# One transformer block on one core: matmul passes that read their 512 weight columns alternately from two halves

## The chip, the core and the metric

The kernel runs on one core of a Trainium2 chip. Each core has a matrix engine (TensorE; PE in the profile, with PEld for its loading of the stationary operand), VectorE (DVE), ScalarE (ACT), GpSimd (POOL) and SyncE (SP), which here only starts transfers. The metric is the device time of one execution in microseconds. Before the change it is 292.63 us, the median of 3 runs (292.62 to 293.44).

## The reference

One block of depth 1 on an input of 256 tokens by 1024 channels, all in 32-bit floats. Cut to what matters:

```python
u = rms_norm(h, mix_norm_g[l])
proj = u @ w_in[l]                                  # 1024 x 2560
q, k, v, glu_a, glu_g = jnp.split(proj, splits, axis=-1)
attn_out = moba_attention(heads(q), heads(k), heads(v), rel_bias)
conv_out = conformer_conv(glu_a, glu_g, conv_w[l], conv_b[l], conv_ln_g[l], conv_ln_b[l])
h = h + jnp.concatenate([attn_out, conv_out], axis=-1) @ w_out[l]
u = rms_norm(h, ffn_norm_g[l])
h = h + (jax.nn.silu(u @ w_gate[l]) * (u @ w_up[l])) @ w_down[l]
return rms_norm(h, final_norm_g)
```

The feed-forward width is 2816, so gate and up are 1024 x 2816 each and down is 2816 x 1024. With 256 tokens the attention has a single block, and is plain causal attention with a position bias, 8 heads of 64.

## The kernel before

**Split weights, three passes.** Each weight arrives as 32-bit floats in a tile `raw` (128 x 1024). `high` (line 138) rounds it on ScalarE to a tile `wh` of the shorter float type fp32r, and `split` (line 158) subtracts on VectorE, leaving the rest in a part `wl` of one long tile, `low`. Activations are split likewise (`uh`, `ul` and `hh`, `hl`, all within the tile `us`; `fh`, `fl` for the feed-forward's products). A product is three passes of TensorE into one accumulator: high by high, high by low, low by high. `cut` (line 165) gives the columns of `wh` and `wl` for a pass.

**Which operand moves.** A pass holds one operand of 128 columns still and streams the other through. For q, k, the convolution's inputs and the output projection the weights are held and 256 columns of activations move. For values (`v_mm`, line 460), gate and up (`up_mm`, line 579) and down (`down`, line 636) the activations are held, 128 tokens at a time, and **512 columns of weights move**; the result has tokens on its partitions. Down has a few passes of 256 columns too, at the very end (accumulator `pe`).

**The columns' layout.** The host function `_layout` (line 794) arranges the weights. For values a row holds 8 stretches of 512 columns, one for each 128 input channels. For gate and up such a stretch is 256 columns of gate followed by 256 of up, for one group of the feed-forward width; for down it is half of a row of 1024. Each pass reads its 512 columns one after another, 4 bytes each.

**Order.** Up to the feed-forward part the order of the work is written out by hand in `PROGRAM` (line 43), a list of steps; each engine runs its steps in that order. The values' steps `v.0` to `v.3` stand among the steps of the softmax and the convolution; each is 12 passes. Then 11 groups follow (line 673): for group g, `swiglu` turns the accumulators `pf` of gate and up into products `ff`; `gate_up` issues the 48 passes of the next group (8 blocks of input channels, 2 blocks of tokens, 3 passes each); the 24 passes of `down` for group g - 1 follow, into the four accumulators `pd`; the splits of the weights for two groups later are queued on ScalarE and VectorE. All passes are recorded at line 74 (transposes at line 77) and all instructions of the other engines at line 85, so that the tiles' names tell them apart. At the end (line 697) the last three down groups are ordered by token half, with the residual sum, the final norm and the output behind each half.

**Transfers.** Weights come in transfers of 512 KB (256 KB for the first ones) on SyncE's queue, into 6 `raw` buffers, two for each weight; `wh` has 9 buffers and `wl` 9 places.

Of the kernel before, what the change touches and what calls it, by code (L numbers as in the profile page):

```python
# [15 lines left out]
P = 128  # L16
S = 256
D = 1024
# [43 lines left out]
def block_kernel(ctx, tc, xT, w_in, w_out, w_gu, w_down, pvec, gfin, relb, hot, out):  # L62
# [10 lines left out]
    def mm(*args, **kw):  # L73
        return tc.keep_in_program_order(nc.tensor.matmul(*args, **kw))  # L74
# [14 lines left out]
    def bank(i, name):  # L89
        return psum.tile([P, 512], F32, tag=f"b{i}", name=name)  # L90
# [15 lines left out]
    raws, parts = {}, {}  # L106
# [58 lines left out]
    def cut(name, c, n):  # L165
        return [w[:, c % HW : c % HW + n] for w in parts[name][c // HW]]


    def mm3(o, name, c, uh, ul, start, stop):
        wh, wl = cut(name, c, P)  # L170
        mm(o, wh, uh, start=start, stop=False, skip_group_check=True)
        mm(o, wh, ul, start=False, stop=False, skip_group_check=True)
        return mm(o, wl, uh, start=False, stop=stop, skip_group_check=True)
# [286 lines left out]
    def v_mm(i):  # L460
        if i == 0:
            pvt.extend(bank(t, f"pv{t}") for t in range(2))
        for k in range(2 * i, 2 * i + 2):
            wh, wl = cut(f"v{k // 4}", (k % 4) * 512, 512)
            for t in range(2):
                tok = slice(t * P, (t + 1) * P)
                mm(pvt[t], uh[:, k, tok], wh, start=k == 0, stop=False)
                mm(pvt[t], uh[:, k, tok], wl, start=False, stop=False)
                mm(pvt[t], ul[:, k, tok], wh, start=False, stop=k == KD - 1)
# [85 lines left out]
    def a0(k):  # L555
# [6 lines left out]
    ops = {"ld": fetch, "zd": bias_out, "bd": bias_in, "ud": stack_out, "us": stack_in, "h": high, "w": split, "rb": row_scale, "hb": bias_parts, "pl": late_columns, "pz": bias_mm, "zs": bias_copy, "vt": v_out, "rs": scale_x, "rd": scale_diagonal, "ca": lambda half: conv_taps(half, 0, 1),  # L562
           "a0": a0, "a1": a1, "glu": glu, "qk": qk_mm, "qo": qk_out, "sc": score, "t": logits, "n": normed, "fl": flip,
           "fo": flip_out, "v": v_mm, "pv": pv_mm, "mo": mix_out, "l": norm, "o": o_mm, "f": finish, "c": conv,
           "co": conv_out, "cw": conv_weights, "ct": conv_taps, "hs": lambda m: sumsq(acch, xs[:, m], m, "h"),
           "sq": lambda k: sumsq(accx, xs[:, k], k, "x"), "g": lambda m: lower_u(m, PV_G2)}
# [10 lines left out]
    pf, ff, acts = {}, {}, {}  # L577

    def up_mm(g, t, k):
        wh, wl = cut("gu"[k // 4] + str(g), k % 4 * 512, 512)  # L580
        tok = slice(t * P, (t + 1) * P)
        mm(pf[g][t], hh[:, k, tok], wh, start=k == 0, stop=False)
        mm(pf[g][t], hh[:, k, tok], wl, start=False, stop=False)
        mm(pf[g][t], hl[:, k, tok], wh, start=False, stop=k == KD - 1)

    def gate_up(g):
        pf[g] = [bank(next(spare), f"pf{g}{t}") for t in range(2)]
        for k in range(KD):
            for t in range(2):
                up_mm(g, t, k)  # L590
# [44 lines left out]

    def down(g, i, t, lo, hi, o=None, start=None, stop=None):
        f = 2 * g + i
        wh, wl = cut(f"d{g}", i * D + lo, hi - lo)
        fh, fl = (a[:, t, i] for a in acts[g])
        if o is None:  # L640
            o = pd[t][lo // 512][:, lo % 512 : lo % 512 + hi - lo]
            start, stop = f == 0, f == (NF - 1 if lo == 0 else NF - 3)
        mm(o, fh, wh, start=start, stop=False, skip_group_check=True)
        mm(o, fh, wl, start=False, stop=False, skip_group_check=True)
        mm(o, fl, wh, start=False, stop=stop, skip_group_check=True)
# [17 lines left out]
    for k in range(KD):  # L663
        for t in range(2):
            up_mm(0, t, k)
        if k == 5:
            rc2 = rstd(acch, D, RMS_EPS, "h", next(spare))
            split("u1")
# [4 lines left out]
    for g in range(FG):  # L673
        swiglu(g)
        if g < FG - 1:
            send(g)
            gate_up(g + 1)
        if g > 0:
            split(f"d{g - 1}")
            land(g - 1)  # L680
        if 0 < g < FG - 2:
            for i in range(2):
                for t in range(2):
                    for n in range(2):
                        down(g - 1, i, t, n * 512, n * 512 + 512)
        if g < FG - 2:
            split(f"g{g + 2}")
            split(f"u{g + 2}")
        if 1 <= g <= 4:
            h_turn(2 * g - 2)  # L690
            h_turn(2 * g - 1)
        if g == 4:
            h_rows()
# [3 lines left out]
    for i in range(2):  # L697
        for t in range(2):
            for n in range(2):
                down(FG - 3, i, t, n * 512, n * 512 + 512)  # L700
        flip_ff(FG - 1, i)

    def last(g, t, lo, hi, *o):
        for i in range(2):
            down(g, i, t, lo, hi, *((o[0], i == 0, i == 1) if o else ()))

    a, b = FG - 2, FG - 1
# [54 lines left out]
def _one_hot():  # L762
    hot = np.zeros((2, NB, S), np.float32)
    hot[:, _buckets(), np.arange(S)] = float(HD) ** 0.5
    return hot.reshape(2 * NB, S)
# [3 lines left out]
def _conv_taps(w):  # L769
    return w[: 4 * Q].reshape(Q, 4, 16, 32).transpose(1, 3, 2, 0).reshape(P, 16 * Q)  # L770


def _pieces(w, fine=0):
    j = [*range(0, fine, HW // 2), *range(fine, w.shape[1] + 1, HW)]
    return np.concatenate([w[:, a:b].ravel() for a, b in zip(j, j[1:])])


def _rows(w):
    k = w.shape[0] // P
    return w.reshape(k, P, w.shape[1]).transpose(1, 0, 2)  # L780
# [3 lines left out]
def _rows_d(w):  # L784
    return w.reshape(4, KD, 32, w.shape[1]).transpose(0, 2, 1, 3).reshape(P, KD, w.shape[1])

def _turned(w):
    g = w[: FF - S].reshape(FG - 1, 4, 2, 32, D).transpose(0, 2, 1, 3, 4).reshape(FF - S, D)  # L790
    return np.concatenate([g, w[FF - S :]], axis=0)


def _layout(x, mix_norm_g, w_in, rel_bias, conv_w, conv_b, conv_ln_g, conv_ln_b, w_out,
            ffn_norm_g, w_gate, w_up, w_down, final_norm_g):
    flat = lambda a: np.ascontiguousarray(a.reshape(P, -1))
    wi = _rows_d(w_in[0])
    q, k, v, a, g = (wi[:, :, i * 512 : (i + 1) * 512] for i in range(5))
    parts = []
    for half in range(2):  # L800
        c = slice(half * S, (half + 1) * S)
        parts.append(np.concatenate([a[:, :, c], g[:, :, c]], axis=2).reshape(P, -1))
    for hp in range(4):
        c = slice(hp * P, (hp + 1) * P)
        parts.append(np.concatenate([q[:, :, c], k[:, :, c]], axis=2).reshape(P, -1))
    parts.append(v.reshape(P, -1))
    pairs = [_rows_d(w[0]).reshape(P, KD, FG, S).transpose(0, 2, 1, 3) for w in (w_gate, w_up)]
    cols = lambda b: b.reshape(-1, P).T
    pvec = np.concatenate(
        [_rows_d(mix_norm_g[0][:, None])[:, :, 0], _rows_d(ffn_norm_g[0][:, None])[:, :, 0], cols(conv_b[0]), cols(conv_ln_g[0]), cols(conv_ln_b[0]),  # L810
         *(cols(w) for w in conv_w[0][4 * Q :]), _conv_taps(conv_w[0]), np.tile(np.eye(32, dtype=np.float32), (4, 1))], axis=1)
    return {
        "xT": np.ascontiguousarray(_rows_d(np.ascontiguousarray(x[0].T)).transpose(1, 0, 2)),
        "w_in": _pieces(np.concatenate(parts, axis=1), 2048 * len(FINE)),
        "w_out": _pieces(flat(_rows(w_out[0].reshape(D, 4, KD, 32).transpose(0, 2, 1, 3).reshape(D, D)))),
        "w_gu": _pieces(flat(np.concatenate(pairs, axis=3))),
        "w_down": _pieces(flat(_rows(_turned(w_down[0])))),
        "pvec": np.ascontiguousarray(pvec),
        "gfin": np.ascontiguousarray(final_norm_g),
        "relb": np.ascontiguousarray(rel_bias),  # L820
        "hot": _one_hot(),
    }
# [17 lines left out]
```

## Time and profile before

| | |
|---|---|
| median of 3 runs | 292.63 us |
| span of the profiled execution | 291.1 us |
| TensorE busy | 283.6 us, 97% of the span |
| VectorE, ScalarE busy | 203.6 us, 156.7 us |
| mean granted clock of TensorE | 0.997 |
| bytes moved by the DMA engines | 63.73 MB, mean 219 GB/s |

The span runs from the first to the last instruction; the profile gives no other time for that execution, and the median of the runs is 1.5 us above the span. "Busy" counts TensorE's passes with a modelled end, and passes overlap, so a busy TensorE need not be at its best pace: the pace is the time from the start of one pass to the start of the next. A group of instructions is listed as line, engine, operation, output<-inputs, shape and count, then busy us, mean ns of one, and idle time before. The granted clock is a share of 2.4 GHz; the other level is 1.2 GHz.

### The profile page before, as it was taken

How to read it: one execution, taken by the hardware profiler on the slowest of the kernel's cores; microseconds unless marked ns; L12 is line 12 of the kernel's file. 1: busy time of each engine (PE TensorE's matmuls, PEld its weight loads, DVE VectorE, ACT ScalarE, POOL GpSimd, SP SyncE). 2: the span in 40 equal slices, each digit the busy share in tenths (PEclk: the TensorE clock that was granted, in tenths of full speed). 3: DMA queues.
4: the chain of work that ended last, by engine and by line, in shares of the span. 5: the costliest groups of instructions: out<-in, count | busy, mean ns of one | idle time of the engine just before them, and what ended most of it. 6: DMA issues, size and time to landing. Idle time of an engine off the chain costs nothing.

```text
span 291.1 us, 4726 instructions
## 1 busy us (share of the span) xinstructions
PE 283.6 (97%) x1717; PEld 243.4 (84%) x1717; DVE 203.6 (70%) x375; ACT 156.7 (54%) x272; POOL 43.6 (15%) x80
## 2 busy tenths in 40 slices
PE   8999999999999999999999999999999999999991
PEld 8999996986799988888888888888888888888881
DVE  3998998999986989859928467381829365411884
ACT  3984668916795577547618173452618172402531
POOL 2000100000000002143211213223221213130000
PEclk9999999999999999999999999999999999999998
DMA  7999799951057447989994949889795949420012
GB/s 221 332 379 335 252 275 252 385 194 55 16 160 260 175 140 205 328 274 303 347 311 148 297 117 321 292 266 356 237 266 172 296 117 325 134 74 0 0 55 89
DMA packets 22089, 63.73 MB, mean 219 GB/s; under 512 B 3178, under 2 KB 5938, under 8 KB 22066
## 3 DMA queue, kind: packets, MB, share of 16 engines
q1 hardware_dynamic: 18754, 54.94, 57.5%
q0 software_dynamic: 2880, 7.95, 9.7%
q10 hardware_dynamic: 432, 0.54, 0.5%
q8 instruction: 13, 0.21, 0.3%
q14 instruction: 10, 0.08, 0.1%
HBM read 58.10 MB, written 5.32 MB: 218 GB/s over the span
## 4 chain that ended last, share of the span: by engine, by line
PE 92%; issue 2%; DVE 2%; DMA 2%; SPq 1%; ACT 1%; POOLq 0%; POOL 0%; DVEq 0%
PE pf L74 41%; PE pd L74 18%; PE py L74 8%; PE pqk L74 8%; PE pv L74 4%; PE pa L74 3%; PE pg L74 3%; PE pc L74 3%; DMA raw_a<-in_w_in 2%; PE pt L77 1%; PE ps L74 1%; PE po L74 1%; DVE ht L85 1%; SPq L85 1%; DVE hg L85 0%
## 5 line engine op out<-in xcount | busy, mean ns | idle before, releaser
L74 PE MATMUL pf<-wl,us 128*128 128x512 f32 x176 | 68.5, 389 | 0.0
L74 PE MATMUL pf<-wh_u,us 128*128 128x512 f32 x176 | 56.2, 390 | 0.0
L74 PE MATMUL pf<-wh_g,us 128*128 128x512 f32 x176 | 56.0, 389 | 0.0
L85 DVE TENSOR_TENSOR ff<-fs,pf 128x256 f32<-128x256 f32 x22 | 9.1, 419 | 55.4 <-ACT fs L85 55.4
L85 ACT ACTIVATE fs<-pf,rc_h 128x256 f32<-128x256 f32 x22 | 10.3, 475 | 67.3 <-PE pf L74 65.8
L74 PEld LDWEIGHTS pf<-wl,us 128*128 128x128 f32 x176 | 33.0, 188 | 6.9
L74 PEld LDWEIGHTS pf<-wh_u,us 128*128 128x128 f32 x176 | 33.0, 188 | 6.8
L74 PEld LDWEIGHTS pf<-wh_g,us 128*128 128x128 f32 x176 | 33.0, 188 | 6.8
L74 PE MATMUL pd<-wh_d,fh 128*128 128x512 f32 x84 | 32.9, 391 | 0.0
L74 PE MATMUL pd<-wh_d,fl 128*128 128x512 f32 x84 | 32.7, 390 | 0.0
L74 PE MATMUL pd<-wl,fh 128*128 128x512 f32 x84 | 32.7, 389 | 0.0
L85 DVE TENSOR_TENSOR wl<-raw_u,wh_u 128x1024 fp32r<-128x1024 f32 x22 | 26.5, 1220 | 8.7 <-ACT wh_u L85 8.7
L85 ACT CAST wh_u<-raw_u 128x1024 fp32r<-128x1024 f32 x22 | 22.8, 1051 | 14.6 <-PE pf L74 10.9
L85 POOL DMA_DIRECT2D fb<-fd x40 | 23.2, 585 | 45.1 <-issue 23.5
L85 DVE TENSOR_TENSOR wl<-raw_g,wh_g 128x1024 fp32r<-128x1024 f32 x22 | 25.9, 1217 | 1.0 <-ACT wh_g L85 1.0
L85 DVE TENSOR_TENSOR wl<-raw_d,wh_d 128x1024 fp32r<-128x1024 f32 x22 | 25.6, 1202 | 0.5 <-ACT wh_d L85 0.5
L74 PE MATMUL pqk<-us,wh_qk 128*128 128x256 f32 x128 | 22.2, 277 | 0.0
L85 ACT CAST wh_g<-raw_g 128x1024 fp32r<-128x1024 f32 x22 | 22.0, 1049 | 0.0
L85 ACT CAST wh_d<-raw_d 128x1024 fp32r<-128x1024 f32 x22 | 21.9, 1047 | 0.0
L74 PEld LDWEIGHTS pqk<-us,wh_qk 128*128 128x128 f32 x128 | 19.4, 188 | 0.5 <-issue 0.4
L74 PEld LDWEIGHTS pd<-wh_d,fl 128*128 128x128 f32 x84 | 15.8, 188 | 3.3
L74 PEld LDWEIGHTS pd<-wl,fh 128*128 128x128 f32 x84 | 15.8, 188 | 3.2
(153 smaller groups left out, 531.9 us busy)
## 6 DMA issues: line engine op xcount, KB each, us to landing
raw_g<-in_w_gu SPq DMA_DIRECT2D x22, 512.0 KB, 5.3
raw_u<-in_w_gu SPq DMA_DIRECT2D x22, 512.0 KB, 6.5
raw_d<-in_w_down SPq DMA_DIRECT2D x22, 512.0 KB, 5.1
raw_qk<-in_w_in SPq DMA_DIRECT2D x8, 512.0 KB, 7.5
raw_o<-in_w_out SPq DMA_DIRECT2D x8, 512.0 KB, 4.2
raw_a<-in_w_in SPq DMA_DIRECT2D x12, 256.0 KB, 4.3
fd<-fv POOLq DMA_DIRECT2D x10, 256.0 KB, 3.9
fb<-fd POOLq DMA_DIRECT2D x40, 64.0 KB, 4.9
```

What stands on the lines that cost most here:

```text
L74: return tc.keep_in_program_order(nc.tensor.matmul(*args, **kw))
L77: return tc.keep_in_program_order(nc.tensor.transpose(o, i, ident))
L85: return lambda *a, **k: tc.keep_in_program_order(f(*a, **k))
```

## The change

In the kernel a view is laid over the 512 columns of a moving weight. `in_turns` takes them as two halves of 256 and walks column 0 of the first half, column 0 of the second, column 1 of the first, column 1 of the second, and so on. On the host `_in_turns` stores the columns of each stretch of 512 so that this walk meets them in their old order: even columns fill the first half and odd ones the second. So the results stand in the same places in the accumulators as before. For down's passes of 256 columns the view is cut to the matching 128 columns of each half.

```diff
+    def in_turns(w):
+        return w.rearrange("p (h a) -> p a h", h=2)
 
@@ v_mm
-            wh, wl = cut(f"v{k // 4}", (k % 4) * 512, 512)
+            wh, wl = map(in_turns, cut(f"v{k // 4}", (k % 4) * 512, 512))
@@ up_mm
-        wh, wl = cut("gu"[k // 4] + str(g), k % 4 * 512, 512)
+        wh, wl = map(in_turns, cut("gu"[k // 4] + str(g), k % 4 * 512, 512))
@@ down
-        wh, wl = cut(f"d{g}", i * D + lo, hi - lo)
+        a, b = lo % 512 // 2, (lo % 512 + hi - lo) // 2
+        wh, wl = (in_turns(w)[:, a:b] for w in cut(f"d{g}", i * D + lo // 512 * 512, 512))
@@ host
+def _in_turns(w):
+    return w.reshape(*w.shape[:-1], -1, S, 2).swapaxes(-1, -2).reshape(w.shape)
...
-    parts.append(v.reshape(P, -1))
+    parts.append(_in_turns(v).reshape(P, -1))
...
-        "w_gu": _pieces(flat(np.concatenate(pairs, axis=3))),
-        "w_down": _pieces(flat(_rows(_turned(w_down[0])))),
+        "w_gu": _pieces(flat(_in_turns(np.concatenate(pairs, axis=3)))),
+        "w_down": _pieces(flat(_rows(_turned(_in_turns(w_down[0]))))),
```

`S` is 256. No instruction is added, removed or moved on any engine, and the transfers keep their sizes and order; the held operand, the accumulators and the splitting of the weights are as before. The passes for q, k, the convolution's inputs and the output projection are not touched.

## The prediction

> **What bounds the kernel now.** I read the page first: the busy shares, then the chain that ended last.
>
> ```profile
> PE 283.6 (97%) x1717; PEld 243.4 (84%) x1717; DVE 203.6 (70%) x375; ACT 156.7 (54%) x272; POOL 43.6 (15%) x80
> PE 92%; issue 2%; DVE 2%; DMA 2%; SPq 1%; ACT 1%; POOLq 0%; POOL 0%; DVEq 0%
> PE pf L74 41%; PE pd L74 18%; PE py L74 8%; PE pqk L74 8%; PE pv L74 4%; PE pa L74 3%; PE pg L74 3%; PE pc L74 3%; DMA raw_a<-in_w_in 2%; PE pt L77 1%; PE ps L74 1%; PE po L74 1%; DVE ht L85 1%; SPq L85 1%; DVE hg L85 0%
> ```
>
> TensorE is busy for 97% of the span, and 92% of the chain is TensorE. The three tiles that the change touches, pf (gate and up), pd (down) and pv (values), are 41 + 18 + 4 = 63% of it. So what counts is how fast one such pass follows the next. The groups, each shape apart, give the number of passes:
>
> ```profile
> L74 PE MATMUL pf<-wl,us 128*128 128x512 f32 x176 | 68.5, 389 | 0.0
> L74 PE MATMUL pf<-wh_u,us 128*128 128x512 f32 x176 | 56.2, 390 | 0.0
> L74 PE MATMUL pf<-wh_g,us 128*128 128x512 f32 x176 | 56.0, 389 | 0.0
> L74 PE MATMUL pd<-wh_d,fh 128*128 128x512 f32 x84 | 32.9, 391 | 0.0
> L74 PE MATMUL pd<-wh_d,fl 128*128 128x512 f32 x84 | 32.7, 390 | 0.0
> L74 PE MATMUL pd<-wl,fh 128*128 128x512 f32 x84 | 32.7, 389 | 0.0
> L74 PE MATMUL pv<-wh_v,us 128*128 128x512 f32 x32 | 10.6, 398 | 0.0
> L74 PE MATMUL pv<-wl,us 128*128 128x512 f32 x16 | 6.3, 392 | 0.0
> L74 PE MATMUL pe<-wl,fh 128*128 128x256 f32 x8 | 2.3, 283 | 0.0
> ```
>
> That is 3 x 176 = 528 passes for pf, 3 x 84 = 252 for pd and 48 for pv, each of 512 columns, together 828; and three groups of 8 = 24 passes of 256 columns into pe (one of the three is shown). The mean of 389 ns is the length of one pass from its start to its modelled end; passes overlap, so it is not the pace. The pace comes from the chain of waits in order of time (start, length, what, number of passes):
>
> ```profile
> 52.43 1.31 PE pt L77 x12
> ...
> 90.48 13.62 PE py L74 x120
> ...
> 137.25 5.44 PE pd L74 x24
> 142.69 10.88 PE pf L74 x48
> ```
>
> Gate and up: 10.88 us / 48 = 226.7 ns a pass. Down: 5.44 / 24 = 226.7 ns. The passes of 256 columns into py: 13.62 / 120 = 113.5 ns, half of it. So the pace goes by the column, 0.443 ns each, and there is no visible fixed part for a pass. The granted clock says what a cycle is:
>
> ```profile
> core 0: 291.1 us, clock 0.997
> ```
>
> At the upper level, 2.4 GHz, 512 cycles are 213.3 ns. A pass of 226.7 ns is 544 cycles: **one cycle lost for every 16 columns**. Who takes that cycle? The windows give an answer (length; busy us and number of instructions of PE, PEld, DVE, ACT, POOL; granted clock, DMA share, GB/s):
>
> ```profile
> 70.70:76.40 5.70, 5.70 (x29) 4.62 (x26) 5.57 (x18) 4.49 (x12) 0.00 (x0) 1.00 0.00 0
> ...
> 137.25:153.57 16.32, 16.32 (x74) 13.51 (x73) 10.06 (x17) 7.46 (x10) 3.20 (x5) 1.00 0.97 317
> ...
> 251.49:267.80 16.31, 16.31 (x74) 13.50 (x73) 4.42 (x9) 3.45 (x6) 3.21 (x5) 1.00 0.13 33
> ```
>
> The last two rows hold the same 72 passes (48 + 24). In one the DMA engines are 97% busy and VectorE works 10.06 us; in the other 13% and 4.42 us. The time is 16.32 and 16.31 us. So neither transfers nor the other engines take the cycle; it belongs to TensorE's own reading or writing. Is it fixed, though? The timeline of the end says no:
>
> ```profile
> 277.70 0.28 PE L74 MATMUL pe<-wh_d,fh 128*128 128x256 f32 x1
> 277.82 0.28 PE L74 MATMUL pe<-wl,fh 128*128 128x256 f32 x1
> ...
> 279.14 0.40 PE L74 MATMUL pd<-wh_d,fh 128*128 128x512 f32 x1
> ```
>
> Twelve passes of 256 columns start between 277.70 and 279.14: 1.44 / 12 = 120 ns each, 288 cycles, two lost in 16, where py's same shape loses one. The column count does not set the loss, then; something about what is read when does. The transposes into pt are the third case: 1.31 us / 12 = 109.2 ns for 128 columns, two cycles a column (106.7 ns) and 2.5 ns beside it. Read at half the pace, they show no loss of a sixteenth, which would be 6.7 ns.
>
> **The change, part by part.** It adds, removes and moves no instruction; each engine has the order that it had, and every load, rounding and subtraction has the same size. Only the order differs in which those 828 + 24 passes walk through their moving operand, and the host's layout that makes up for it. So splits, transfers and all other engines are costed at nothing, and what is left is one unknown: the pace of a pass that takes column 0 of one half, column 0 of the other half 1 KB further on, then column 1 of the first, and so on.
>
> No row of this trace has such a pass, so I bound it. From below: 512 cycles, 213.3 ns; I assume that no more than one column a cycle goes in, and no row shows more. From above: two cycles a column, as in the transposes, 109.2 x 4 = 437 ns. Between them lie 226.7 ns (nothing changes) and 240 ns (two cycles lost in 16, as in pe). I take **215.8 ns**, no lost cycles but the transposes' 2.5 ns for the instruction. The reason is the comparison above: adjacent columns at one a cycle lose a cycle in 16, and columns at one in two cycles lose none. In turns of one, each half is walked at one column in two cycles, the pace at which the trace has no loss. This is an inference from unlike operations, not a measurement.
>
> The sum, with 226.7 - 215.8 = 10.9 ns a pass:
> - pf: 528 x 10.9 = 5.76 us. TensorE has no gap here, so all of it counts.
> - pd: 252 x 10.9 = 2.75 us, likewise.
> - pe: 24 passes from 120 to 109.2 ns are 0.26 us; I count 0.2, since VectorE's rows at the end run close behind them.
> - pv: 48 x 10.9 = 0.52 us. VectorE is busy for 5.57 of 5.70 us in the values' window, so I count half, 0.26 us.
>
> Sum 8.97, say 9.0 us. The span is 291.1 and the median of the runs 292.63, 1.5 more, which I leave as it is: 292.6 - 9.0 = **283.6 us**.
>
> Is there cover for it, that is, do the others keep up when TensorE wants its operands 4 to 5% sooner? The waits (total us, times, longest):
>
> ```profile
> ACT fs L85 <- PE pf L74: 65.8, 20, 12.7
> ...
> ACT wh_u L85 <- PE pf L74: 10.9, 7, 1.7
> ```
>
> ScalarE waits for TensorE for 65.8 us before the sigmoid products and 10.9 us for a free weight buffer, never the other way in the feed-forward part. A group's period would go from 16.32 to 16.32 - 72 x 0.0109 = 15.54 us; VectorE needs at most 10.06 and ScalarE 7.46 of it. In the values' part the next things late would be the transposes and what stands behind them:
>
> ```profile
> 71.51 2.88 ACT L85 ACTIVATE p<-p,rs 128x128 f32<-128x128 f32 x8 [0.68 <-DVE rs L85]
> ...
> 76.30 1.47 PE L77 MATMUL pt<-ident,p 128*128 128x128 f32 x12
> ```
>
> The last p is there at 71.51 + 2.88 = 74.39, 1.9 us ahead of the transposes; pulling those 0.26 us forward (24 passes stand there) meets no wait at them. What follows them depends on VectorE's queue, hence the half.
>
> **A rule that speaks against it.** The page's figure for the pace first: the Trainium skill, TensorE: Matmul & The Clock Gate, Back-to-back issue gap, gives a warm isolated pass N / 2.4 + 2.5 ns, 215.8 ns at 512 columns. The 226.7 ns here do not agree with it, the transposes' extra 2.5 ns do; by it alone the sum would be the 9.0 us above. On the other side the Trainium skill, SBUF — State Buffer, Door 1 (the note on cachelines), says that SBUF has lines of 16 bytes, that an access in the same line goes at full speed, that at least two hits in a line are needed to hide the memory's latency, and that each access to a new line pays. It gives no price. Adjacent 4-byte columns hit a line four times; in turns of one with 1 KB between, no two successive columns share a line. No run here has shown such a pass, so the trace neither confirms nor refutes it. By that rule the time would rise; the first rival is this, priced from rows.
>
> **The rivals.**
> 1. *Every column a new fetch, and it cannot be had each cycle: slower.* Place: the moving read of the 852 passes. Price by the transposes' two cycles a column: 437 - 226.7 = 210 ns x 828 = 174 us, and pe 24 x (218 - 120) ns = 2.4 us, so about 469 us. It decides as soon as a pass takes over 226.7 ns; the mildest form, two lost in 16 as in pe, is 240 - 226.7 = 13.3 ns x 828 = 11 us, 303.6 us. For it: the trace's two clean cases of fast reading are adjacent columns only. Against it: pe shows the reading's loss to vary for the same columns, so the reading looks ahead over more than one column.
> 2. *The loss belongs to the total stream, not to each half: no change.* If a lost cycle comes with every 64 bytes handed over, wherever they come from, a pass stays at 226.7 ns and the time at 292.6 us. For it: 113.5 against 226.7 ns, an exact proportion to the column count. Against it: pe again.
> 3. *Half of the loss goes,* because each half loses one in its own 16 columns and the two losses fall together: 6.7 ns x 780 = 5.2 us, and 0.4 us for pv and pe: 287.0 us. I count this as the weak end of the forecast.
>
> **How the numbers follow.** The forecast with its weak end: 0.62. It reaches from 281.3 us (213.3 ns: 13.3 x 780 = 10.4 us, and 0.9 us for pv in full and pe) to 287.0. No change: 0.18. Slower in either form: 0.20, mostly the dear one, since a read that cannot be had each cycle is late for every column. A measurement of this kernel can tell about 0.3% (0.9 us) from no change; hence 0.62 faster, 0.18 within, 0.20 slower. The range takes in the forecast and no change, 281.0 to 293.6, and leaves out the slower fifth; 303.6 and 469 are too far apart for a range to hold part of them with meaning.
>
> **What would show it.** Right: in the chain, pf's 48 passes take 48 x 215.8 ns = 10.36 us instead of 10.88, and pd's 24 take 5.18 instead of 5.44; the group's period is near 15.5 us; py and pqk, whose moving operand is not touched, stay at 113 to 120 ns; VectorE's and ScalarE's rows keep their lengths. Rival 2 shows 10.88 again. Rival 1 shows 11.5 (240 ns) or 21 us (437 ns). Wrong in another way would be a pace that falls while gaps open at the start of a group, with a wait for wl or wh: then the cover that I claimed is not there.

## The result, and the profile after

The changed kernel takes **284.61 us** (284.56 to 284.82, 4 runs) against 292.67 us, 8.06 us less; the ratio is 0.9722, with a 95% interval from 0.9709 to 0.9736. The forecast was 283.6 us. Its profiled execution has a span of 283.0 us. The page's busy row and chain, to be laid beside those of before:

```profile
PE 274.6 (97%) x1717; PEld 244.4 (86%) x1717; DVE 203.0 (72%) x375; ACT 156.2 (55%) x272; POOL 43.6 (15%) x80
PE 77%; DVE 10%; issue 4%; DMA 4%; SPq 2%; ACT 1%; POOLq 0%; DVEq 0%; POOL 0%; ACTq 0%
```

The busy time of TensorE's passes fell by 9.0 us. Its weight loading (PEld) rose by 1.0 us, the other engines changed by no more than 0.6, and the counts are the same. But the span fell by only 8.1 us, and the chain, 92% TensorE before, is now 77% TensorE and 10% VectorE: in places another engine has become the later one. The pace stands in the chain in order of time:

```profile
54.03 2.59 PE pv L74 x12
...
90.33 13.63 PE py L74 x120
...
135.88 5.18 PE pd L74 x24
141.06 10.36 PE pf L74 x48
```

2.59 / 12, 5.18 / 24 and 10.36 / 48 are all 215.8 ns a pass, where it was 226.7 in pf and pd: at the upper clock level (granted clock 0.994 after, 0.997 before) 518 cycles for 512 columns instead of 544. The passes into py, which the change does not touch, keep their pace: 13.63 / 120 = 113.6 ns, 113.5 before. A group's period in the windows (columns as before) is 15.54 us instead of 16.32, with the other engines as busy as ever:

```profile
150.24:165.78 15.54, 15.54 (x74) 13.61 (x73) 9.75 (x14) 7.43 (x10) 3.21 (x5) 1.00 0.88 248
```

**Where the gain came from, and where some of it went.** Five starts in the timeline cut the span into six pieces; the fifth is VectorE's first residual sum (ht<-pd), and the lines below it show the end of the last piece. Before:

```profile
53.50 0.48 PE L74 MATMUL pv<-wh_v,us 128*128 128x512 f32 x1
...
103.94 0.39 PE L74 MATMUL pf<-wh_g,us 128*128 128x512 f32 x1
...
137.09 0.39 PE L74 MATMUL pd<-wh_d,fh 128*128 128x512 f32 x1
...
267.65 0.39 PE L74 MATMUL pd<-wh_d,fh 128*128 128x512 f32 x1
...
276.61 0.75 DVE L85 SCALAR_TENSOR_TENSOR ht<-pd,rc_h,ht 128x512 f32<-128x512 f32 x1 [1.36 <-PE pd L74]
...
284.56 0.28 PE L74 MATMUL pe<-wh_d,fl 128*128 128x256 f32 x1
...
284.88 0.48 DVE L85 SCALAR_TENSOR_TENSOR ht<-pe,rc_h,ht 128x256 f32<-128x256 f32 x1
```

After:

```profile
53.79 0.46 PE L74 MATMUL pv<-wh_v,us 128*128 128x512 f32 x1
...
103.78 0.38 PE L74 MATMUL pf<-wh_g,us 128*128 128x512 f32 x1
...
135.72 0.38 PE L74 MATMUL pd<-wh_d,fh 128*128 128x512 f32 x1
...
260.04 0.38 PE L74 MATMUL pd<-wh_d,fh 128*128 128x512 f32 x1
...
268.61 0.75 DVE L85 SCALAR_TENSOR_TENSOR ht<-pd,rc_h,ht 128x512 f32<-128x512 f32 x1 [0.96 <-PE pd L74]
...
276.08 0.28 PE L74 MATMUL pe<-wh_d,fl 128*128 128x256 f32 x1
276.31 0.48 DVE L85 SCALAR_TENSOR_TENSOR ht<-pe,rc_h,ht 128x256 f32<-128x256 f32 x1
...
276.77 0.47 DVE L85 SCALAR_TENSOR_TENSOR ht<-pe,rc_h,ht 128x256 f32<-128x256 f32 x1
```

| piece | before, us | after, us | gained | by 10.9 ns a pass, as forecast |
|---|---|---|---|---|
| up to the first pv pass (none changed) | 53.50 | 53.79 | -0.29 | 0 |
| to the first pf pass (48 passes of pv) | 50.44 | 49.99 | 0.45 | 0.26 (half counted; 0.52 in full) |
| to the first pd pass (144 of pf) | 33.15 | 31.94 | 1.21 | 1.57 |
| to the first pd pass of the third last group (576) | 130.56 | 124.32 | 6.24 | 6.28 |
| to the first residual sum (36 of pd) | 8.96 | 8.57 | 0.39 | 0.39 |
| to the end (24 of pd, 24 of pe) | 14.49 | 14.39 | 0.10 | 0.46 |
| sum | 291.10 | 283.00 | 8.10 | 8.96 |

In the long middle the gain is whole, and the values' passes (pv) brought nearly all of theirs. It is short in three places. Two of them show in the waits (total, times, longest):

```profile
PEld ps_h L74 <- DVE acch L85: 0.5, 1, 0.5
...
PEld ps_x L74 <- DVE accx L85: 0.4, 1, 0.4
```

The first row stood at 0.2 us before. In the first group the passes ahead of the small sum ps_h are done sooner, but VectorE's running sum acch is not, and TensorE stands still for half a microsecond. The second row is missing before, but nothing points to the change as its cause. It lies ahead of every changed pass; `before_held_at_0` below, whose weights are walked as before, has the same row at 0.3 us and starts its first pv pass at 53.78, as late as here; and `sum_later`, whose weights are walked in turns, has no such row and starts it at 53.33. That start varies from execution to execution. The third place is the end. Before, VectorE took up its last residual sum (284.88) as the last pass ended (284.56 + 0.28 = 284.84). Now that pass ends at 276.36, but VectorE starts the sum before it only at 276.31 and gets to the last one at 276.77. From VectorE's first residual sum to this point 8.27 us passed before and 8.16 now: its own work there had almost no room to give.

### The profile page after: what moved, and what is told of

Same layout as the page of the kernel before. It is cut to its first block, busy times and chain, and to the rows that moved or that the text cites. A ratio compares the mean times of both kernels' runs of the same rounds, so it can differ in the third digit from the quotient of the medians.

```text
span 283.0 us, 4726 instructions
## 1 busy us (share of the span) xinstructions
PE 274.6 (97%) x1717; PEld 244.4 (86%) x1717; DVE 203.0 (72%) x375; ACT 156.2 (55%) x272; POOL 43.6 (15%) x80
## 4 chain that ended last, share of the span: by engine, by line
PE 77%; DVE 10%; issue 4%; DMA 4%; SPq 2%; ACT 1%; POOLq 0%; DVEq 0%; POOL 0%; ACTq 0%
PE pf L74 38%; PE pd L74 17%; PE pqk L74 8%; PE py L74 8%; DMA raw_a<-in_w_in 4%; DVE cacc L85 3%; SPq L85 2%; DVE wl L85 2%; PE pc L74 2%; DVE acch L85 1%; PE pa L74 1%; PE pg L74 1%; PE pv L74 1%; DVE accx L85 1%; DVE ht L85 1%
## 5 line engine op out<-in xcount | busy, mean ns | idle before, releaser
L74 PE MATMUL pf<-wl,us 128*128 128x512 f32 x176 | 66.7, 379 | 0.0
L74 PE MATMUL pf<-wh_u,us 128*128 128x512 f32 x176 | 54.4, 379 | 0.0
L74 PE MATMUL pf<-wh_g,us 128*128 128x512 f32 x176 | 54.1, 379 | 0.0
L85 ACT ACTIVATE fs<-pf,rc_h 128x256 f32<-128x256 f32 x22 | 10.3, 473 | 56.9 <-PE pf L74 55.5
L74 PE MATMUL pd<-wh_d,fh 128*128 128x512 f32 x84 | 32.0, 381 | 0.0
L74 PE MATMUL pd<-wh_d,fl 128*128 128x512 f32 x84 | 31.9, 380 | 0.0
L74 PE MATMUL pd<-wl,fh 128*128 128x512 f32 x84 | 31.8, 379 | 0.0
L74 PE MATMUL py<-mh,wh_o 128*128 128x256 f32 x64 | 18.1, 282 | 0.0
L74 PE MATMUL py<-ml,wh_o 128*128 128x256 f32 x64 | 17.8, 278 | 0.3 <-DVE ml L85 0.3
```

Of the source, the lines that this page charges most:

```text
L85: return lambda *a, **k: tc.keep_in_program_order(f(*a, **k))
```

## The experiments

All but `before_held_at_0`, `sum_later` and `acts_too` change one thing: the order in which a pass walks its 512 stored columns, with the host's layout to match. Each is the changed kernel with another view in `in_turns` (the cut for pe is adapted). The reading of their results is gathered behind them.

**Turns of sixteen.**

```diff
-        return w.rearrange("p (h a) -> p a h", h=2)
+        return w.rearrange("p (h a n) -> p a h n", h=2, a=16, n=16)
```

> The walk takes 16 adjacent columns (64 bytes) of the first half, then 16 of the second, and so on; all else as in the changed kernel. Theory HALF PACE (the prediction's: a stretch of memory walked at one column in two cycles loses nothing, adjacent columns at one a cycle lose one in 16): inside a stretch the columns are adjacent again, so a pass goes back to 226.7 ns, a group of 72 passes to 16.32 us, the time to about 292.6 us. Theory DISTANCE (what helps is that the two halves lie 1 KB apart, so that neighbouring stretches come from different places of the memory): 215.8 ns and about 284.6 us.

Measured: 303.35 us, ratio 1.0367 (1.0337 to 1.0397). The chain has

```profile
145.26 11.52 PE pf L74 x48
```

that is 240 ns a pass, two cycles lost in 16: dearer than adjacent columns. DISTANCE falls: the halves still lie 1 KB apart, and the gain is gone. HALF PACE has the direction (no gain), not the size: it said 226.7.

**Turns of one between neighbours 64 bytes apart.**

```diff
+        return w.rearrange("p (b h a) -> p b a h", b=16, h=2, a=16)
```

> Turns of one, but between two stretches of 16 columns that are neighbours (64 bytes apart), within each 32 columns. HALF PACE: 215.8 ns a pass, 284.6 us, as the changed kernel. DISTANCE: 226.7 ns or more, 292.6 us.

Measured: 284.37 us, ratio 0.9719 (0.969 to 0.9747).

```profile
140.57 10.36 PE pf L74 x48
```

215.8 ns: a distance of 64 bytes does what 1 KB does. DISTANCE falls for good.

**One stream in steps of two.**

```diff
+        return w.rearrange("p (h a) -> p a h", h=256, a=2)
```

> One stream in steps of two columns (8 bytes): the even places of the 512, then the odd ones. Each 64 bytes are now passed in 8 cycles, twice. HALF PACE says that what is walked faster loses more: a lost cycle for every 64 bytes passed, 2 in 16, 240 ns a pass, about 303 us. Theory NEIGHBOURS (the loss comes only from two successive columns that lie side by side): 215.8 ns, 284.6 us. Theory LINES (a line of 16 bytes must be hit at least twice in a row to go at full pace; two hits here): no dearer than 226.7 ns, 292.6 us.

Measured: 483.53 us, ratio 1.6525 (1.6477 to 1.6573).

```profile
191.94 21.76 PE pf L74 x48
```

453.3 ns, 1088 cycles, twice the 544 of adjacent columns. All three theories miss it. HALF PACE, the prediction's own reason, named a sixteenth more and got a factor of two.

**One stream in steps of four.**

```diff
+        return w.rearrange("p (h a) -> p a h", h=128, a=4)
```

> One stream in steps of four columns (16 bytes), four walks over the 512: no two successive columns within 16 bytes of each other, and 128 columns between two visits to the same 16 bytes. HALF PACE: a lost cycle for every 64 bytes passed, here every 4 columns, 5/4 of 213.3 = 267 ns, about 292.6 + 828 x 0.040 = 326 us. NEIGHBOURS: 215.8 ns, 284.6 us. LINES: one hit a visit, so every column pays; at two cycles a column as in the transposes 437 ns, about 469 us.

Measured: 489.16 us, ratio 1.6717 (1.6669 to 1.6766).

```profile
193.22 22.14 PE pf L74 x48
```

461.3 ns. HALF PACE (267) and NEIGHBOURS (215.8) fall; LINES is near with 437, but LINES had no room for step_2's 453.

**Turns of one between neighbours 16 bytes apart.**

```diff
+        return w.rearrange("p (b h a) -> p b a h", b=64, h=2, a=4)
```

> Turns of one between neighbouring stretches of 4 columns (16 bytes apart): within each 8 columns the walk is 0 4 1 5 2 6 3 7. Successive columns lie as far apart as in step_4, but each 16 bytes is used four times within 8 columns. Theory REUSE (what is fetched must be used again soon, and then it doesn't matter in which of two places it lies): 215.8 ns a pass, 10.36 us for 48, 284.5 us. Theory PLACES (two successive columns can be had together only from the same 8 bytes or from places at least 64 bytes apart): as step_4, about 461 ns a pass, 22.1 us for 48, 489 us.

Measured: 284.11 us, one run.

```profile
140.35 10.36 PE pf L74 x48
```

215.8 ns, as REUSE says; PLACES falls.

**One stream in steps of sixteen.**

```diff
+        return w.rearrange("p (h a) -> p a h", h=32, a=16)
```

> One stream in steps of 16 columns (64 bytes), 32 columns to a walk over the 512, 16 walks: successive columns 64 bytes apart as in near_16, but each piece is used once a visit and seen again only 32 columns later. REUSE: as dear as step_4 or dearer, at least 461 ns a pass, 489 us or more. PLACES: 215.8 ns, 284.5 us.

Measured: 465.85 us, one run.

```profile
187.06 20.80 PE pf L74 x48
```

433.3 ns. PLACES falls a second time; REUSE has the direction, and its bound of 461 ns is missed by 28.

**Turns of two.**

```diff
+        return w.rearrange("p (h a n) -> p a h n", h=2, a=128, n=2)
```

> Two adjacent columns of the first half, two of the second, and so on. REUSE: 215.8 ns a pass, 10.36 us for 48, 284.5 us, since both places are used again and again. Theory SINGLE (the gain needs successive columns from different places every time; each adjacent pair brings back what adjacent columns lose): 226.7 ns, 10.88 us for 48, 292.6 us, or 240 ns as with turns of 16, 303 us.

Measured: 382.05 us, one run.

```profile
165.72 16.00 PE pf L74 x48
```

333.3 ns. REUSE in its plain form and SINGLE both fall: two columns a turn are far dearer than one a turn or sixteen a turn.

**The held operand moved, adjacent columns.** The kernel before, with the activations of gate and up 64 bytes lower:

```diff
-    u_x, u_h = (... for i in (0, SHIFT))
+    u_x, u_h = (... for i in (0, 0))
```

> The kernel before (adjacent columns), with the held activations of gate and up 16 columns (64 bytes) lower, at the start of their tile; nothing else changes. Theory MEETING (the lost cycle in 16 comes from the moving read meeting the reading of the held operand, so it depends on where the two lie to each other): the gate and up passes change, to 213.3 or to 240 ns, 10.2 or 11.5 us for 48, while down's stay at 226.7; about 286 or 300 us. Theory OWN (the moving read loses it by itself): 226.7 ns everywhere, 292.6 us.

Measured: 294.31 us, one run, beside 292.67 us for the kernel before.

```profile
143.28 10.99 PE pf L74 x48
154.27 5.44 PE pd L74 x24
```

229.0 ns in pf, in each of eight groups, and 226.7 in pd as ever. So where the held operand lies does matter, by 2.3 ns a pass for this one shift. The lost cycle in 16 (13.3 ns) neither went nor doubled, as MEETING had it; OWN is nearly right. Other shifts were not tried.

**Turns of one from four quarters.**

```diff
+        return w.rearrange("p (h a) -> p a h", h=4, a=128)
```

> Turns of one from four quarters of 128 columns. Theory TWO READERS (formed on the runs so far: the even and the odd columns of a walk are fetched apart, each side holds the 16 bytes that it fetched last, and what counts is how many columns in a row that side takes from them: four in near_4 and near_16, two with adjacent columns, one in step_2, step_4 and step_16): each side now changes its place at every column, so a pass is as dear as in turns_of_2 or step_2, 333 to 461 ns, 16.0 to 22.1 us for 48, 382 to 489 us. REUSE: each piece is used four times within 16 columns, 215.8 ns, 284.5 us.

Measured: 339.92 us, one run.

```profile
154.79 13.60 PE pf L74 x48
```

283.3 ns: dearer than turns of one from two places, as TWO READERS says and REUSE does not, but below the 333 ns that TWO READERS had as its least.

**Turns of one from two halves, each in steps of two.**

```diff
+        return w.rearrange("p (h a c) -> p c a h", h=2, c=2)
```

> Turns of one from two halves, but in steps of two columns within each half: 0 256 2 258 4 260 and so on, then the odd places. TWO READERS, where the count of columns from one fetch sets the loss: two for each side as with adjacent columns, so 226.7 to 240 ns a pass, 10.88 to 11.52 us for 48, 292.6 to 303 us. Theory SHARED (adjacent columns lose because both sides want the same 16 bytes, which they don't here): 215.8 ns, 284.5 us. Theory STEP (any step over one column within a stream is dear, as in step_2): 453 ns, about 483 us.

Measured: 292.54 us, one run.

```profile
142.40 10.88 PE pf L74 x48
```

226.7 ns, to the digit the pace of adjacent columns, as TWO READERS had it at its lower end. SHARED and STEP fall.

**What the walks say together.** Take the even and the odd columns of a walk as two sequences, and count how many columns in a row each takes from the same 16 bytes:

| walk | in a row | ns a pass |
|---|---|---|
| turns of one, halves (the change); near_16; near_4 | 4 | 215.8 |
| adjacent (before); halves_step_2 | 2 | 226.7 |
| turns_of_16 | 2, with a jump every 8 | 240 |
| quarters | 1, two places in turn | 283.3 |
| turns_of_2 | 1, two places in turn | 333.3 |
| step_16, step_2, step_4 | 1 | 433.3, 453.3, 461.3 |

The count puts the walks in order: four in a row cost 215.8 ns, two 226.7 to 240, one 283 to 461. It was formed on the earlier runs, so what tests it are the last two: halves_step_2, chosen to have adjacent columns' count with another geometry, came out as foretold, and quarters got its direction but not its size. The numbers of the count can also be held against its nearest rivals. Without the two sequences, the change, near_4 and step_4 all take one column in a row, and they cost 215.8, 215.8 and 461.3 ns. With 8 bytes in place of 16, adjacent columns and step_2 would both count one (226.7 and 453.3); with 32 bytes, adjacent columns and near_4 would both count four (226.7 and 215.8).

Three things stay open. Where each side has two places in turn, the walks cost 1.3 and 1.6 cycles a column, while the other walks with a count of one cost two or a little more; so more than the last 16 bytes seems to be held, and the two cases differ. turns_of_16 is dearer than adjacent columns with the same count; its jumps are the difference, but near_4, which moves on after every four columns, loses nothing. And before the change the passes of 256 adjacent columns into pe lost two cycles in 16 (120 ns), where pf with the same count lost one; in the changed kernel they take 111.7 ns. Whether the place of the held operand is the reason, as in before_held_at_0, was not tried. That there are two sides inside the engine is argued from these paces and not seen.

The Trainium skill, SBUF — State Buffer, Door 1 (the note on cachelines), asks for at least two hits in a 16-byte line: step_2 has two in a row and is dear, and the change has one and is fast. So the rule agrees with these runs only when it is counted for each side, and two hits still cost the sixteenth that four don't.

**The new wait taken away.**

```diff
-        if k == 5:
+        if k == 6:
             rc2 = rstd(acch, D, RMS_EPS, "h", next(spare))
             split("u1")
```

The splitting of a weight that stands behind the sum moves along, but in between only TensorE has instructions, so the order on the other engines stays.

> The changed kernel, with the four small passes that sum the squares over partitions (ps_h) one block of input channels later in the first gate and up group (after 42 passes, not 36). If what the change gave back there is TensorE's new wait for VectorE's running sum acch (0.5 us in the waits), the first pd pass comes 0.3 to 0.5 us sooner: 284.1 to 284.3 us. If VectorE's or ScalarE's queues set the pace there anyway, or the wait moves to the products of group 0: 284.6 us.

Measured: 283.89 us (283.77 to 284.01, 4 runs), ratio 0.9698 (0.9682 to 0.9714). The start of the first pf pass in the timeline, and the first pd piece of the chain:

```profile
103.33 0.38 PE L74 MATMUL pf<-wh_g,us 128*128 128x512 f32 x1
```

```profile
112.56 0.34 PE ps_h L74 x4
112.90 22.12 PE pf L74 x102
135.02 5.18 PE pd L74 x24
```

From the first pf pass to the first pd pass it takes 135.02 - 103.33 = 31.69 us, by the same two rows 135.88 - 103.78 = 32.10 us in the changed kernel: 0.41 us back, and the four small passes have their 0.34 us again. TensorE's wait on acch is gone from the list. So the shortfall in the first group was this wait. The median fell by 0.72 us, more than that. In the profiled executions 0.46 us was there before the first pv pass (53.79 against 53.33), ahead of the edit: the late start of the changed kernel's profiled execution. near_16 and near_4, without this edit, start that pass at 53.31 and 53.13 too. So only the 0.41 belongs to the edit.

**The activations' passes in turns as well.** On top of sum_later. One of the three places where such passes are issued, and one of the three where VectorE reads their results:

```diff
-            w, u = ..., (ul if n == 1 else uh)[:, k]
+            w, u = ..., in_turns((ul if n == 1 else uh)[:, k])
...
-        part = lambda p, j: p[half][:, j * S : (j + 1) * S]
+        part = lambda p, j: p[half][:, j * S : (j + 1) * S].rearrange("p (a h) -> p h a", h=2)
```

> The kernel of sum_later, and the 576 passes of 256 columns of activations into pa, pg, pqk and py read in turns of one from two halves as well; the results then stand in turns in the accumulators, and VectorE reads them in steps of two columns there (and takes four more instructions for q and k). By the pace of pe in the changed kernel, about 111 ns against 113.4: 576 x 2.4 ns = 1.4 us less than sum_later, 282.8 us. If VectorE, which is busy for most of that part, sets its pace, or reads the accumulators slower in steps: no gain or up to 2 us more than sum_later.

Measured: **283.18 us** (283.01 to 283.26, 5 runs), ratio 0.9673 (0.9657 to 0.9688), the fastest of all. Its chain, and VectorE's rows for reading the accumulators in steps (line, engine, operation, shapes, count, busy, mean ns):

```profile
10.55 0.67 PE pa L74 x6
...
30.97 12.10 PE pqk L74 x106
...
89.30 13.50 PE py L74 x120
```

```profile
L85 DVE TENSOR_TENSOR xs<-py,xs 128x256 f32<-128x256 f32 x8 | 3.3, 417 | 0.2 <-PE py L74 0.2
```

Passes of 256 columns take 0.67 / 6 = 111.7 ns into pa, where the kernel before has 0.68 / 6 = 113.3, and 13.50 / 120 = 112.5 into py against 113.5. VectorE's reading in steps costs nothing measurable: 417 ns each, 418 in the changed kernel. Half of the expected 1.4 us came: 0.71 us between the medians, and in the profiled executions the first pf pass starts at 102.63 instead of 103.33. The pace got 1.0 to 1.6 ns better, not 2.4, and for q and k it is 12.10 / 106 = 114.2 ns, hardly better than the 13.81 / 120 = 115.1 of the changed kernel. The intervals of the two ratios overlap a little, but all five runs (283.01 to 283.26) lie below all four of sum_later (283.77 to 284.01).

## Why the prediction was right, point by point

- **The pace, 215.8 ns: right to the digit,** in pf, pd and pv. The bound from below (213.3) was not reached; the 2.5 ns taken from the transposes stand.
- **The reason given for it was half right.** The prediction said that a stretch of memory walked at one column in two cycles loses nothing. That holds for the change and for near_16 and near_4, but as a rule it fails: it gave 226.7 ns for turns_of_16 (240 measured), 240 for step_2 (453) and 267 for step_4 (461), and turns_of_2, which on average also passes each half at half pace, takes 333. So the right pace was in part luck. What the runs showed in its place: it isn't the speed at which a stretch is passed, but how many columns in a row the even and the odd sequence each take from the same 16 bytes. Turns of one raise that from two to four.
- **The sum: 9.0 us forecast, 8.06 measured between the medians, 8.10 between the spans.** pf and pd in the long middle gave 6.24 of 6.28. Too large were two terms: pf, where 0.4 us of the 5.76 went into the wait of ps_h for acch (shown by sum_later, 0.41 back), and pd with pe at the end, where 0.36 of 0.46 was lost because VectorE became the later engine. Too small was pv: 0.26 was counted, because VectorE is so busy there, and 0.45 of the full 0.52 came. sum_later, near_16 and near_4 agree: from the first pv pass to the first pf pass they take 50.00, 50.00 and 49.95 us, the kernel before 50.44. The 0.29 us of the late start belong to no term.
- **"Do the others keep up": right in the groups, wrong at the edges.** The row on which it rested, ScalarE's wait for TensorE, stands at 55.5 us after, 65.8 before; so there was slack in the groups, before and after. But the prediction looked for late operands only in the groups and at the values' transposes. The first group's sum over partitions, where TensorE needs something of VectorE's, was not looked at: the pf term counts in full on the ground that TensorE has no gap there, which the faster passes changed. The end was seen, and still counted nearly in full.
- **pe from 120 to 109.2 ns: 2.5 ns short.** In the changed kernel twelve such passes start from 269.63 on and the next pass at 270.97, 111.7 ns each.
- **Rival 1 (slower)** did not happen, but its mechanism exists: steps of four make a pass 461 ns and the kernel 489.16 us, against the 437 ns and 469 us of its price. By the count above it decides when each side finds only one column in a row in 16 bytes; in turns of one it finds four.
- **Rival 2 (no change)** and **rival 3 (half the loss)** did not happen: the passes into pf, pd and pv got rid of all of their 26 extra cycles (544 to 518).

## What to carry to other kernels

Where TensorE is the bound, take the time from the start of one pass to the start of the next, turn it into cycles by the granted clock, and compare it with the columns: here 544 cycles for 512 columns of 4 bytes showed a loss that no busy share tells. With 4-byte columns, turns of one between two runs of adjacent columns (as near as 16 bytes) bring it to 518 cycles; steps of two or more in one stream, turns of two and four places in turn cost 283 to 461 ns a pass, so a view over a moving operand has to be measured before it is kept. After such a gain look at the points where the faster engine waits for a sum or a running total of another, which sit at the edges of stages and not in the steady part.

## What had not been expected of the hardware

- Steps of two columns cost exactly twice adjacent columns (1088 cycles against 544), and turns of two 333.3 ns, while turns of one between places 16 bytes apart are the fastest walk seen (215.8 ns).
- Moving the held operand by 64 bytes changes a pass with adjacent columns from 226.7 to 229.0 ns (one run).
- VectorE reads an accumulator in steps of two columns at the same length as adjacent ones (417 and 418 ns for 128 x 256).
